# Modulation rows of a two-layer recurrent backbone: spaced differently under the mixers, a quarter under the out-projection, loaded on GpSimd's queue

## The chip, the cores and the metric

The kernel runs on one core of one Trainium2 chip. The metric is the device time of one execution in microseconds (us), the median of several runs; lower is better. The engines are TensorE (PE, with its weight loads as PEld), VectorE (DVE), ScalarE (ACT), GpSimd (POOL) and SyncE (SP). SP computes nothing here: it issues DMAs, in order, and holds at the first one whose buffer is not free yet.

## What is computed

Two layers work on 256 context tokens and 1024 latent tokens of width 1024, all in float32. Each layer is a mixing sub-layer (four groups of heads: HGRN2, mLSTM, retention, GLA, each scanned forwards and backwards, then one out-projection) and a squared-ReLU MLP. Both are modulated by vectors made from a conditioning vector, one for the latent tokens (`c`) and one for the context (`c_ctx`):

```python
def modulate(x, shift, scale):
    return rmsnorm(x) * (1.0 + scale) + shift

mod_l = (jax.nn.silu(c) @ w_ada[layer] + b_ada[layer])[:, None, :]
mod_c = (jax.nn.silu(c_ctx) @ w_ada[layer] + b_ada[layer])[None, None, :]
sh1_l, sc1_l, g1_l, sh2_l, sc2_l, g2_l = jnp.split(mod_l, 6, axis=-1)
xl = xl + g1_l * mixer_out(raw_l, pl, g_heads[layer], w_out[layer])
xl = xl + g2_l * sq_relu_mlp(modulate(xl, sh2_l, sc2_l), w_ff1[layer], w_ff2[layer])
```

## The kernel before, in words

Activations lie with the channels on the 128 partitions and the 1280 tokens along the free dimension, in three token blocks: 256 context columns, then twice 512. Every matrix product is done as three float32r products (`mm3`, lines 293 to 296), with each operand split into a high and a low part. A weight half is loaded raw by SP (line 281), its high part is copied by ACT (282), its low part is subtracted by DVE (283).

The modulation of layer 0's first sub-layer (part r = 0) is made by TensorE at the start. The other parts are made by **modulation rows** in `ada_rows`: for each token kind j, each half h of the 1024 inputs and each of 16 blocks o of 128 outputs, a DMA brings 128 rows of `w_adaR`, 512 wide (256 KB, line 413), and one DVE instruction multiplies them with the conditioning half `c` and accumulates along the free dimension (line 414). `c` is itself a DMA of `d_c`, broadcast to 128 partitions (line 410). Before the change all these DMAs stand on SP's queue, between its weight loads, stores and fetches.

Where rows are made:

- Under the mixers of layer 0 (`mixers`): parts r = 1 and 2 of layer 0, 128 rows, with two row buffers and one conditioning buffer from the heap. The mixers' own steps are generators that `Fill.along` interleaves with dense projections. Each step of a projection is a fill step, and on three of every five of them one row is emitted (`self.n % 5 in (0, 2, 4)`). The order of phases is GLA, HGRN2 (two head pairs), mLSTM, retention.
- Under the MLP of layer 0: parts r = 0, 1, 2 of layer 1, 128 rows, from the generator `ada1`, which `filler` advances three times after each of the 32 hidden tiles. It has five row buffers and one conditioning buffer, so each change of half waits until the last product with the old half is done, and then for a load.

```python
ring = Ring(ws[2 * o:2 * o + 2]) if o < fixed else rest
u = self.wtile(self.io["w_out"][l, o], ring)
```

The out-projection (`outproj`) keeps the weights of its first `fixed` output blocks in place for all three token blocks, and streams the others through a ring of three slots, again for each token block. With 13 slots `fixed` is 5.

What a line emits is only a wish: a scheduler at build time puts each engine's instructions in their final order, and may put a row's product earlier or later among DVE's instructions than its place in the program. Each engine then executes its own list strictly in that order. DVE operations of HGRN2 that matter below are the exponent differences and masked copies of `mix_vec` (lines 919 to 1038), which feed PE.

## Time and profile before

| what | value |
|---|---|
| median of 3 runs (lowest, highest) | 3276.86 us (3276.39, 3285.53) |
| the profiled execution's own time | 3277.57 us |
| its span, first to last instruction | 3275.8 us |
| mean granted TensorE clock | 0.990 |
| busy: PE, DVE, ACT, POOL | 97%, 64%, 39%, 0% |

The mixers of layer 0 take the time from about 55 to 760 us of the span, its out-projection goes on to 918 us, its MLP to about 1790 us; then layer 1 follows in the same order, without rows. PE is the engine that is nearly always busy, so what counts is where it stands idle and where its granted clock is below 1.00. The view by windows gives both for any stretch; the view of waits names what PE waited for.

### The profile page before, as it was taken

The page shows a single profiled execution, that of the slowest core. Times are in us where ns is not written, and L with a number is a line of the kernel's source. Part 1 is how long each engine was busy: PE and PEld are TensorE (multiplying, and loading weights), DVE is VectorE, ACT ScalarE, POOL GpSimd, SP SyncE. Part 2 cuts the span into 40 slices and gives each one's busy share as a digit, 9 for nine tenths or more (in the row PEclk, how much of TensorE's full clock was granted, in tenths as well). Part 3 has the DMA queues.
Part 4 walks back from the last instruction along what each step waited for, and adds up shares of the span by engine and source line. Part 5 has one row for each costly group of instructions (what it writes and reads, how often), then busy time and mean ns, then how long its engine had stood idle before and what let it go on. Part 6 is the DMA issues. An engine that isn't in the chain of part 4 may idle for free.

```text
span 3275.8 us, 52563 instructions
## 1 busy us (share of the span) xinstructions
PE 3188.0 (97%) x20681; PEld 2607.3 (80%) x20681; DVE 2098.3 (64%) x4333; ACT 1285.0 (39%) x2665; POOL 11.5 (0%) x42
## 2 busy tenths in 40 slices
PE   7999999999999999999999999999999999999998
PEld 4787788878888888888888677788778888888887
DVE  4778887776588845454545586876756555555546
ACT  4666564545332121212122575764444322222222
POOL 0000000000000000000000000000000000000000
PEclk9999899999999999999999999999999999999999
DMA  6115566345157511111111212333224111111111
GB/s 208 58 61 176 183 186 190 120 134 179 63 165 230 161 39 39 39 39 39 39 39 40 78 64 73 120 109 113 90 72 151 58 46 52 46 52 46 52 49 65
DMA packets 181953, 308.20 MB, mean 94 GB/s; under 512 B 21880, under 2 KB 51240, under 8 KB 181448
## 3 DMA queue, kind: packets, MB, share of 16 engines
q1 hardware_dynamic: 180376, 303.02, 28.8%
q8 instruction: 162, 2.65, 0.3%
q10 hardware_dynamic: 1296, 1.81, 0.2%
q14 instruction: 87, 0.71, 0.1%
q0 software_dynamic: 32, 0.01, 0.0%
HBM read 259.11 MB, written 45.65 MB: 93 GB/s over the span
## 4 chain that ended last, share of the span: by engine, by line
PE 81%; DVE 8%; DMA 6%; ACT 3%; issue 1%; SPq 0%; DVEq 0%; ACTq 0%
PE psum L294 22%; PE psum L295 21%; PE psum L296 21%; PE psum L831 2%; PE psum L601 2%; PE psum L834 1%; PE psum L818 1%; PE psum L632 1%; DMA ph<-w_adaR 1%; PE psum L634 1%; PE psum L633 1%; PE psum L1359 1%; PE psum L706 1%; PE psum L1019 1%; DMA ps<-w_ada 1%
## 5 line engine op out<-in xcount | busy, mean ns | idle before, releaser
L526 DVE SCALAR_TENSOR_TENSOR x<-psum,st,x 128x512 f32<-128x512 f32 (+1 forms) x648 | 440.7, 689 | 203.5 <-PE psum L296 202.8
L282 ACT ACTIVATE pc<-st 128x512 fp32r<-128x512 f32 x256 | 161.2, 632 | 854.4 <-PE psum L295 840.9
L295 PE MATMUL psum<-pc,pc 128*128 128x512 f32 (+1 forms) x1296 | 477.0, 368 | 6.0 <-DVE pc L506 6.0
L294 PE MATMUL psum<-pc,pc 128*128 128x512 f32 (+1 forms) x1296 | 476.1, 367 | 0.0
L296 PE MATMUL psum<-pc,pc 128*128 128x512 f32 (+1 forms) x1296 | 474.7, 366 | 0.0
L294 PE MATMUL psum<-Hhi,pc 128*128 128x512 f32 (+1 forms) x1280 | 471.1, 368 | 1.5 <-ACT pc L282 1.5
L295 PE MATMUL psum<-Hlo,pc 128*128 128x512 f32 (+1 forms) x1280 | 472.0, 369 | 0.1
L296 PE MATMUL psum<-Hhi,pc 128*128 128x512 f32 (+1 forms) x1280 | 470.5, 368 | 0.0
L294 PE MATMUL psum<-Hhi,pw 128*128 128x512 f32 (+1 forms) x1192 | 451.5, 379 | 7.6 <-ACT pw L282 3.5
L295 PE MATMUL psum<-Hlo,pw 128*128 128x512 f32 (+1 forms) x1192 | 447.5, 375 | 0.0
L296 PE MATMUL psum<-Hhi,pw 128*128 128x512 f32 (+1 forms) x1192 | 446.6, 375 | 0.6 <-DVE pw L283 0.6
L505 DVE TENSOR_TENSOR st<-st 128x256 f32<-128x256 f32 (+1 forms) x160 | 101.8, 637 | 301.5 <-ACT pc L504 300.8
L295 PEld LDWEIGHTS psum<-pc,pc 128*128 128x128 f32 x1296 | 245.0, 189 | 48.4 <-DVE pc L506 6.9
L294 PEld LDWEIGHTS psum<-pc,pc 128*128 128x128 f32 x1296 | 245.0, 189 | 44.1 <-DVE x L526 1.2
L296 PEld LDWEIGHTS psum<-pc,pc 128*128 128x128 f32 x1296 | 244.6, 189 | 42.9 <-issue 2.7
L294 PEld LDWEIGHTS psum<-Hhi,pc 128*128 128x128 f32 x1280 | 241.3, 189 | 43.3 <-ACT pc L282 2.4
L295 PEld LDWEIGHTS psum<-Hlo,pc 128*128 128x128 f32 x1280 | 241.3, 189 | 41.0 <-issue 0.5
L283 DVE TENSOR_TENSOR pc<-st,pc 128x512 fp32r<-128x512 f32 x256 | 175.6, 689 | 153.4 <-ACT pc L282 133.5
L296 PEld LDWEIGHTS psum<-Hhi,pc 128*128 128x128 f32 x1280 | 241.1, 188 | 41.0 <-DVE pc L283 0.6
L294 PEld LDWEIGHTS psum<-Hhi,pw 128*128 128x128 f32 x1192 | 227.3, 191 | 53.7 <-issue 9.2
L296 PEld LDWEIGHTS psum<-Hhi,pw 128*128 128x128 f32 x1192 | 227.1, 191 | 39.3 <-issue 2.4
L295 PEld LDWEIGHTS psum<-Hlo,pw 128*128 128x128 f32 x1192 | 227.6, 191 | 37.7 <-issue 2.9
(401 smaller groups left out, 4859.4 us busy)
## 6 DMA issues: line engine op xcount, KB each, us to landing
st<-w_ff SPq DMA_DIRECT2D x256, 256.0 KB
ph<-w_adaR SPq DMA_DIRECT2D x128, 256.0 KB
st<-w_inT SPq DMA_DIRECT2D x96, 256.0 KB
st<-w_adaR SPq DMA_DIRECT2D x74, 256.0 KB
pc<-w_adaR SPq DMA_DIRECT2D x54, 256.0 KB
st<-w_out SPq DMA_DIRECT2D x50, 256.0 KB
d_z<-st SPq DMA_DIRECT2D x40, 256.0 KB
ps<-w_ada SPq DMA_DIRECT2D x32, 256.0 KB
```

The source lines that it names most:

```text
L282: nc.scalar.activation(hi, raw, AF.Copy)
L283: (eng or nc.vector).tensor_tensor(lo, raw, F(hi), op=ALU.subtract)
L294: t.matmul(out, lhsT=w[0], rhs=m[0], start=first, stop=False)
L295: t.matmul(out, lhsT=w[0], rhs=m[1], start=False, stop=False)
L296: t.matmul(out, lhsT=w[1], rhs=m[0], start=False, stop=last)
L505: nc.vector.tensor_tensor(r, r, r, op=ALU.mult)
L526: nc.vector.scalar_tensor_tensor(x, ps, self.mod[:, l, 40 + o, j:j + 1], x, op0=ALU.mult, op1=ALU.add)
L601: t.matmul(ps[:, 0:304], lhsT=h[a], rhs=u[b], start=(k + i == 0), stop=(k == NK - 1 and i == 2))
L632: t.matmul(ps[:, e, :], lhsT=h[0], rhs=u[0], start=(k == 0), stop=False)
L633: t.matmul(ps[:, e, :], lhsT=h[0], rhs=u[1], start=False, stop=False)
L634: t.matmul(ps[:, e, :], lhsT=h[1], rhs=u[0], start=False, stop=(k == NK - 1))
L831: nc.tensor.matmul(o, lhsT=ST[r0:r0 + kd, c, d, :], rhs=qd[d](c)[r0:r0 + kd, :], start=(j == 0), stop=False, tile_position=(r0, 0))
```

## The change

Five things are altered.

1. Under the mixers a row is emitted on 5 of every 20 fill steps in HGRN2, and on 11 of 20 from mLSTM on.
2. Half of part r = 2 (output blocks 8 to 15, 32 rows for both token kinds) is left out there and made in the out-projection: none or one row after each context output, two after each 512-column output. Two slots of the out-projection are cut into two row buffers and two conditioning buffers, so that 11 slots are left and `fixed` is 4.
3. In the out-projection and in the MLP both conditioning halves are kept for as long as the token kind stays the same, and the rows alternate between the halves.
4. In the MLP the six buffers are four for rows and two for conditioning, in place of five and one.
5. All row and conditioning DMAs are issued from GpSimd's queue.

```diff
-                self.n += 1
-                if self.also and self.n % 5 in (0, 2, 4):
-                    next(self.also, None)
+                if self.also:
+                    self.due += self.part
+                    if self.due >= 20:
+                        self.due -= 20
+                        next(self.also, None)
...
-            for h in range(2):
-                c = cs.next()(512)
-                queue.dma_start(c.rearrange("p (k q) -> p k q", q=128), self.d_c[j:j + 1, 4 * h:4 * h + 4, :].to_broadcast([128, 4, 128]))
-                for o in range(16):
-                    w = wring.next()(512)
-                    queue.dma_start(w, self.io["w_adaR"][l, r, o, :, 512 * h:512 * h + 512])
-                    nc.vector.scalar_tensor_tensor(w, w, 1.0, c, op0=ALU.mult, op1=ALU.mult, accum_out=S[:, o:o + 1, h])
-                    if o % several == several - 1:
-                        yield
+            if both and self.cond_now != j:
+                self.cond_c = [cond(j, h) for h in range(2)]
+                self.cond_now = j
+            seq = [(h, o) for o in range(o0, o1) for h in range(2)] if both else [(h, o) for h in range(2) for o in range(o0, o1)]
+            for i, (h, o) in enumerate(seq):
+                if both:
+                    c = self.cond_c[h]
+                elif o == o0:
+                    c = cond(j, h)
+                w = wring.next()(512)
+                queue.dma_start(w, self.io["w_adaR"][l, r, o, :, 512 * h:512 * h + 512])
+                nc.vector.scalar_tensor_tensor(w, w, 1.0, c, op0=ALU.mult, op1=ALU.mult, accum_out=S[:, o:o + 1, h])
+                if i % several == several - 1:
+                    yield
...
-            fill.also = ada([ao.sub(512 * i, 512) for i in range(3)])
+            fill.also, fill.part = ada([ao.sub(512 * i, 512) for i in range(3)]), 5
...
+        fill.part = 11
...
-        nslot = (self.rest - NK * NT) // 1024
-        po, ws = self.pool(f"po{l}", [1024] * (nslot - 5))
+        nslot = (self.rest - NK * NT) // 1024 - (0 if l else 2)
+        po, ws = self.pool(f"po{l}", [1024] * (nslot - 5) + [512] * (0 if l else 4))
+        rows = None
+        if l == 0:
+            ab, ws = ws[-4:], ws[:-4]
+            rows = self.ada_rows(0, 2, (0, 1), Ring(ab[:2]), Ring(ab[2:]), nc.gpsimd, o0=8)
+            self.cond_now = None
...
+                if rows:
+                    for _ in range(o % 2 if a < CTX else 2):
+                        next(rows, None)
...
-            for r in (1, 2):
-                yield from b.ada_rows(0, r, (0, 1), Ring(bufs[:2]), Ring(bufs[2:]), nc.sync)
+            for r, n in ((1, 16), (2, 8)):
+                yield from b.ada_rows(0, r, (0, 1), Ring(bufs[:2]), Ring(bufs[2:]), nc.gpsimd, o1=n)
...
+            w4, c2 = Ring(bufs[:-2]), Ring(bufs[-2:])
+            b.cond_now = None
             for r in range(3) if l == 0 else ():
-                yield from b.ada_rows(1, r, (0, 1) if r == 0 else (1,), Ring(bufs[:5]), Ring(bufs[5:]), nc.sync, 2)
+                yield from b.ada_rows(1, r, (0, 1) if r == 0 else (1,), w4, c2, nc.gpsimd, 2)
```

The rest of the diff counts the rows that a part has and adds the bias for that many. Line numbers shift by two at the top (281 to 283 becomes 283 to 285) and by 13 in the middle (`mix_vec`'s line 980 becomes 993). A row's DMA is line 426 then, its product 427, a conditioning load 412.

**DVE, in the middle of HGRN2's first head pair** (the multiplications of line 991, later 1004, and the masked copies of line 1032, later 1045, belong to `mix_vec`; `ph` written together with `st` is a row's product). Before:

```order
L981 TENSOR_TENSOR px_0_693<-px_0_693 128x64x4
L414 SCALAR_TENSOR_TENSOR ph_0_256,st<-ph_0_256 128x512
L991 SCALAR_TENSOR_TENSOR px_0_693<-px_0_693,st 128x512
L414 SCALAR_TENSOR_TENSOR ph_0_256,st<-ph_0_256 128x512
L991 SCALAR_TENSOR_TENSOR px_0_693<-px_0_693,st 128x512
L742 TENSOR_TENSOR st<-st,psum 128x512
L283 TENSOR_TENSOR pw_0_252<-st,pw_0_252 128x512
L1032 COPY_PREDICATED px_0_693<-st,psum 128x256
```

With the change:

```order
L994 TENSOR_TENSOR px_0_693<-px_0_693 128x64x4
L665 TENSOR_TENSOR st<-st 128x256
L1004 SCALAR_TENSOR_TENSOR px_0_693<-px_0_693,st 128x512
L427 SCALAR_TENSOR_TENSOR ph_0_256,st<-ph_0_256 128x512
L1004 SCALAR_TENSOR_TENSOR px_0_693<-px_0_693,st 128x512
L313 SCALAR_TENSOR_TENSOR st<-psum,st 128x512
L285 TENSOR_TENSOR pw_0_252<-st,pw_0_252 128x512
L1045 COPY_PREDICATED px_0_693<-st,psum 128x256
```

Between the same neighbours one product stands where two stood.

**POOL's queue under HGRN2's second head pair** (`spill_v`'s memsets of a column of ones, line 768, later 781, are POOL's only work there before). Before, all ten stand in one row:

```order
L1210 MEMSET ph_0_256 128x16
L768 MEMSET st 128x4 x10
L1291 MEMSET px_0_693 128x65
```

With the change (around the third conditioning load):

```order
L781 MEMSET st 128x4
L426 DMA ph_0_256<-w_adaR 128x512 x3
L781 MEMSET st 128x4
L426 DMA ph_0_256<-w_adaR 128x512 x2
L412 DMA ph_0_256<-d_c 128x512
L426 DMA ph_0_256<-w_adaR 128x512 x2
L781 MEMSET st 128x4 x2
L426 DMA ph_0_256<-w_adaR 128x512 x4
```

The rows stand between memsets that wait for their own buffers.

**SP's queue at the start of the out-projection** (`x_0` to `x_7` are the residual, `w_out` the weights). Before:

```order
L281 DMA st<-w_out 128x512 x2
L1540 DMA x_6_7732<-xT 128x512
L1540 DMA x_7_7733<-xT 128x512
...
L1540 DMA x_7_7733<-xT 128x512
L281 DMA st<-w_out 128x512 x18
```

With the change:

```order
L1552 DMA st<-d_yg 128x512
L1559 DMA x_6_7670<-xT 128x512
L1559 DMA x_7_7671<-xT 128x512
...
L1559 DMA x_7_7671<-xT 128x512
L283 DMA st<-w_out 128x512 x24
```

The loads of the fifth output block's weights (two halves for each of the three token blocks, where two were enough before) now all stand behind the last residual load.

## Rows read from the trace of the kernel before

**Rows 1.** The page: span, then busy time, share and instructions of each engine.

```profile
span 3275.8 us, 52563 instructions
PE 3188.0 (97%) x20681; PEld 2607.3 (80%) x20681; DVE 2098.3 (64%) x4333; ACT 1285.0 (39%) x2665; POOL 11.5 (0%) x42
```

**Rows 2.** Windows: length, busy PE, PEld, DVE, ACT, POOL (instructions), granted clock, DMA share, GB/s.

```profile
294.00:353.00 59.00, 48.78 (x432) 36.26 (x431) 51.39 (x123) 36.04 (x77) 0.00 (x0) 0.83 0.42 135
353.00:563.00 210.00, 203.52 (x1996) 170.61 (x1997) 171.48 (x460) 118.15 (x269) 1.29 (x12) 1.00 0.61 193
563.00:641.00 78.00, 76.31 (x557) 61.38 (x555) 59.82 (x177) 38.50 (x110) 0.24 (x2) 1.00 0.47 144
641.00:691.00 50.00, 45.47 (x293) 36.36 (x291) 42.09 (x115) 25.63 (x72) 0.00 (x0) 0.90 0.44 139
...
760.00:918.00 158.00, 153.62 (x805) 128.53 (x803) 89.90 (x154) 72.26 (x135) 0.00 (x0) 0.99 0.38 125
...
1053.00:1070.00 17.00, 11.59 (x50) 9.57 (x49) 12.79 (x37) 3.61 (x6) 0.00 (x0) 0.80 0.80 243
```

**Rows 3.** PE's waits in 294:353, 641:691 and 918:1123: us in total, times, longest.

```profile
PE psum L956 <- DVE px L935: 3.9, 1, 3.9
...
PE psum L818 <- DVE ph L1135: 2.3, 1, 2.3
PE psum L294 <- DVE st L311: 1.9, 1, 1.9
...
PE psum L295 <- DVE pc L506: 5.4, 1, 5.4
```

**Rows 4.** Windows of the rows' products (line 414): length, DVE busy (instructions), clock, DMA.

```profile
294.00:353.00 59.00, 11.36 (x34) 0.83 0.42 135
353.00:563.00 210.00, 49.65 (x144) 1.00 0.61 193
```

**Rows 5.** The chain of waits in 200:760: shares by line, then pieces (start us, us).

```profile
by line: PE psum L294 12.2%; PE psum L295 11.9%; PE psum L296 11.8%; DMA ph<-w_adaR 6.9%; PE psum L831 5.2%; PE psum L834 3.6%; PE psum L818 3.1%; PE psum L1359 3.1%; DVE ph L414 2.8%; PE psum L706 2.5%; PE psum L1019 2.3%; DVE px L991 2.3%
...
411.35 3.73 DMA ph<-w_adaR
...
433.43 3.04 DMA ph<-w_adaR
```

**Rows 6.** Line 414 in 353:563: instructions, then what its engine's idle time waited for (us, times).

```profile
L414 DVE SCALAR_TENSOR_TENSOR ph<-ph x72: 680/686/695, 355.8 to 553.9; 128x512 f32<-128x512 f32 x72
...
  DMA ph<-w_adaR: 11.0, 17
  DMA ph<-d_c: 1.7, 2
```

**Rows 7.** The same of line 414 in 918:1123, the MLP.

```profile
  DMA st<-d_c: 19.0, 7
  DMA st<-w_adaR: 3.2, 8
```

**Rows 8.** Waits of SP's queue in 227:720.

```profile
SPq L413 <- DVE ph L414: 106.0, 73, 8.0
```

**Rows 9.** Timeline of POOL; landing of its one DMA (line 333); window 0:50.

```profile
24.85 0.64 POOL L333 DMA_DIRECT2D d_c<-st  x1 [24.41 <-DVE st L332]
...
420.66 0.10 POOL L768 MEMSET st<- 128x4 f32 x1 [4.92 <-DMA d_v<-st]
...
DMA to landing us min/median/max: 4.9/4.9/4.9
...
0.00:50.00 50.00, 31.63 (x133) 10.42 (x133) 16.55 (x71) 19.24 (x48) 1.20 (x7) 1.00 0.91 311
```

**Rows 10.** Waits of PE and ACT around the out-projection's first block, and SP's timeline there.

```profile
PE psum L294 <- ACT pw L282: 3.5, 2, 2.7
...
ACT pw L282 <- DMA st<-w_out: 4.5, 2, 4.0
...
809.28 5.52 SPq L1540 DMA_DIRECT2D x<-xT  x10
```

More of the change, by code (lines that the diff above doesn't have):

```diff
@@ L161, in __init__ @@
         self.slots = slots
-        self.q, self.done, self.owed, self.also, self.n = [], 0, 0, None, 0
+        self.q, self.done, self.owed, self.also, self.part, self.due = [], 0, 0, None, 0, 0
     def add(self, *work):
@@ L400, in ada_finish, with ada_rows, cond @@
             nc.vector.tensor_scalar(m, m, 1.0, None, op0=ALU.add)
-    def ada_rows(self, l, r, toks, wring, cs, queue, several=1):
+    def ada_rows(self, l, r, toks, wring, cs, queue, several=1, o0=0, o1=16):
         nc = self.nc
         S = self.mod[:, 1 - l, 0:16, :]
-        for j in toks:
-            for h in range(2):
-                c = cs.next()(512)
-                queue.dma_start(c.rearrange("p (k q) -> p k q", q=128), self.d_c[j:j + 1, 4 * h:4 * h + 4, :].to_broadcast([128, 4, 128]))
-                for o in range(16):
-                    w = wring.next()(512)
-                    queue.dma_start(w, self.io["w_adaR"][l, r, o, :, 512 * h:512 * h + 512])
-                    nc.vector.scalar_tensor_tensor(w, w, 1.0, c, op0=ALU.mult, op1=ALU.mult, accum_out=S[:, o:o + 1, h])
-                    if o % several == several - 1:
-                        yield
-            mo = self.mod[:, l, 16 * r:16 * r + 16, j]
-            nc.vector.tensor_tensor(mo, S[:, :, 0], S[:, :, 1], op=ALU.add)
-            nc.vector.tensor_tensor(mo, mo, self.bada[:, l, 16 * r:16 * r + 16], op=ALU.add)
-            if r in (0, 2):
+        def cond(j, h):
+            c = cs.next()(512)
+            queue.dma_start(c.rearrange("p (k q) -> p k q", q=128), self.d_c[j:j + 1, 4 * h:4 * h + 4, :].to_broadcast([128, 4, 128]))
+            return c
+        both = len(cs.items) > 1
+        for j in toks:
+            if both and self.cond_now != j:
[12 more added lines that the diff above has]
+                    yield
+            mo = self.mod[:, l, 16 * r + o0:16 * r + o1, j]
+            nc.vector.tensor_tensor(mo, S[:, o0:o1, 0], S[:, o0:o1, 1], op=ALU.add)
+            nc.vector.tensor_tensor(mo, mo, self.bada[:, l, 16 * r + o0:16 * r + o1], op=ALU.add)
+            if (r, o0) in ((0, 0), (2, 0)):
@@ L1566, in outproj @@
                 nc.vector.scalar_tensor_tensor(x, ps, self.mod[:, l, 16 + o, j:j + 1], x, op0=ALU.mult, op1=ALU.add)
+                if rows:
+                    for _ in range(o % 2 if a < CTX else 2):
+                        next(rows, None)
             if a != tbs[-1][0]:
                 self.norm_block(l, (a, n), 24, 32, fast=FAST[4])
+        for _ in rows or ():
+            pass
         po.release()
```

## The prediction

> **What bounds the kernel now.** I read the page first. PE is busy for 3188.0 of 3275.8 us [rows 1], so a change can only win where PE stands idle or runs at a lower clock; DVE, at 64% of the whole, seems to have room. But its share is an average, so the next view is the table of windows, cut where the clock falls [rows 2]. From 294 to 353 us, in HGRN2's first head pair, DVE is busy for 51.39 of 59 us, PE for only 48.78, and the granted clock is 0.83. From 641 to 691, in mLSTM's end and retention's start, PE is busy for 45.47 of 50 at 0.90. From 1053 to 1070, in the MLP, PE is busy for 11.59 of 17 at 0.80. These three short stretches are what the rows of modulation can be charged with; the view of PE's waits says why: in all three PE waits for DVE, 3.9 us at once in the first and 5.4 in the third [rows 3]. A clock below 1.00 is time at the lower level, 1.2 GHz in place of 2.4; in each stretch it follows such a wait.
>
> The reader should see next that the rows are in DVE's way twice. Their products take 11.36 us of DVE in the first stretch and 49.65 in the following 210 us [rows 4], and they make DVE wait for their DMAs: 11.0 us in 17 waits there [rows 6]. The chain of waits from 200 to 760 us runs through row DMAs for 6.9% and through products for 2.8% [rows 5]. In the MLP most of the waiting, 19.0 us, is for the conditioning load `d_c` [rows 7].
>
> The sums are made against the profiled execution's own 3277.57 us; the median of the three runs is 0.7 lower. What a measurement of this kernel can tell from no change is about 0.3%, 9.8 us.
>
> **Where the rows go.** Counting products between the same neighbours in the two orders on DVE, I find 10 before 294 us (11 with the change), 16 against 5 in 294 to 353, 73 against 78 in 353 to 563, 7 against 2 in 563 to 641, 13 against none in 641 to 691, and 9 against none after that; 96 remain. So the emission at 5 of 20 steps does not thin out all of HGRN2: the scheduler pulls the later rows forward, into its second half, and clears mLSTM and retention.
>
> **294 to 353 us.** PE's idle time is 59 - 48.78 = 10.2 us, and the clock's shortfall 0.17 x 59 = 10.0, of which 3.9 / 2 = 1.9 falls on the long wait itself and is not lost twice: 8.1. A product costs 49.65 / 72 = 0.69 us. Eleven fewer free 7.6 us of DVE. I take it that PE's idle time shrinks by those 7.6, three quarters of it, and the clock's loss by the same share, 6.0: gain **13.6**, bounds 0 (the wait has another cause) and 18.3.
>
> **563 to 691 us.** The second stretch loses 4.5 us idle and 0.10 x 50 = 5.0 by the clock. All 13 products leave it, so I take 9 of the 9.5. From 563 to 641 PE idles 1.7 us, and five of seven products go: 1. Gain **10**, bounds 0 and 11.2.
>
> **MLP.** Eight conditioning loads through one buffer become four through two. The third stretch loses 5.4 us idle and 0.20 x 17 = 3.4 by the clock. I take **6** of these 8.8, because one change of token kind keeps its load; bounds 0 and 8.8. The row ring falls from five buffers to four. Four buffers give a row every (4.0 + 0.69) / 4 = 1.2 us with the trip assumed below, and 128 rows in the 205 us from 918 to 1123 need one every 1.6, so I cost that at nothing; at the 4.9 us below it still fits (1.4).
>
> **The other queue.** Taking rows off SP frees it of 106.0 us in which it held for a row's buffer [rows 8]. I give that no gain of its own: no wait of PE in these rows ends on a load. On POOL's queue a row is issued behind memsets, and one of these waited 4.92 us for a store [rows 9]; a product then holds DVE, and with it the operations that feed PE. The price that the trace does not show is a row's round trip from POOL. On SP's queue it is 3.04 to 3.73 us where nothing else held it [rows 5]; POOL's only DMA took 0.64 us to issue and 4.9 to land, though to device memory and with the DMA engines 0.91 busy [rows 9]. I take 4.0, nearer to SP's rows because the transfer is the same, and keep 3.04 and 4.9 as bounds.
>
> With two buffers the 78 rows of 353 to 563 come in 39 pairs, and each waits some 0.6 us longer: 23 us. Six conditioning loads there have only two to eight DVE operations between the last product with the old half and the first with the new, where four to thirteen stood before; at 2 us each that is 12. So 35 us of DVE waits replace 12.7 [rows 6]. DVE's work is 171.48 + 5 x 0.69 = 175 of the 210 us, so 35 just fit, but not without harm, as DVE works in order. PE idles 6.5 us there now beside 12.7 of waits, half a microsecond for each; 22 more cost **-11**. Bounds: 0 (trip 3.4 or less) and -41 (trip 4.9: 39 x 1.5 + 6 x 3 = 76.5 of waits, 41.5 more than DVE has free).
>
> The Trainium skill, page “DMA: Bandwidth & Descriptors”, section “Latency and other measured facts”, puts the first byte at about 1 us where GpSimd's software makes the descriptors and 0.6 where hardware does. By its 0.4 us the pairs would wait 16 us, the loads still 12, and the sum would be 3256; no run here shows it yet.
>
> **Out-projection.** Four more weight halves cost DVE 4 x 0.69 us and 32 products 22, all beside 68 us in which DVE idles [rows 2]; without that cover they would cost up to 25. Streamed weights are late in the first block: PE waits 2.7 us once for a copy that waits 4.0 for `w_out`, behind ten residual loads that SP issues over 5.52 us [rows 10]. With the change four context outputs and one of 512 columns stand ahead of that wait, where there were five and two thirds of one, about 1 us less of cover; the load comes some 0.7 earlier, as one pair fewer is ahead. I take **-1**, bounds +2 and -6 (the wait doubles, and so does the clock's loss, 0.01 x 158).
>
> **Sum:** 13.6 + 10 + 6 - 11 - 1 = 17.6 us gained: 3260.0 for the profiled execution, **3259** for the median.
>
> **Rivals.**
>
> *The load only moves.* DVE in 353 to 563 goes from 82% to 83% by work alone and to the brim with waits; the stall of 294 to 353, which came at 87%, then returns a hundred microseconds later. For it: the 78 products there. Against it: 73 stand there already and PE lost 6.5 us. It takes back the 13.6: **3273**, no change.
>
> *All gain, no price.* If POOL's trip is as SP's and the loads are covered, the gains at their upper bounds are 18.3 + 11.2 + 8.8 = 38.3: **3239**. For it: rows no longer hold behind stores on SP. Against it: closer conditioning loads.
>
> *Slower: the trip from POOL.* Of one pair's 210 / 39 = 5.4 us the trip may take 4.7 before two buffers starve DVE. With a trip of 4.9 the 41 us above are lost, and the time is 3277.6 - 29.6 + 1 + 41 = **3290**. It decides at 4.8: there the waits are 39 x 1.4 + 18 = 73 us, 38 over DVE's 35 free, which is the gain of 28.6 and the 9.8 that count. For it: the 4.9 us of the one row there is. Against it: its destination and its crowded engines. The Trainium skill's page “SBUF — State Buffer”, section “SBUF: two separate sides”, has a mechanism that would lengthen the trip: while DVE runs an operation that takes both shared ports, GpSimd cannot write descriptors. No row here shows it.
>
> **How the numbers follow.** Forecast 0.44 (3249 to 3267), the load moves 0.24 (3268 to 3286), all gain 0.17, slower 0.15. Faster by over 0.3% is the first and third, less a hundredth for the forecast's edge: 0.60; the same 0.25; slower 0.15. The range runs from the full gain, 3238, to the upper end of no change, 3287, and leaves out the slow case alone.
>
> **What would show it.** Right: in the new profile the clock stays at 1.00 around 294 to 353 and 641 to 691, PE's waits for lines 935 and 1135 (by their new numbers) are gone or under 1 us, the MLP's waits for `d_c` fall under 6 us, and DVE's waits for row DMAs before 563 are near 35 us. Wrong: a new stretch below 0.9 of the clock between 353 and 563, or in the out-projection; a landing time of POOL's row DMAs above 4.8 us; or a wait on `d_c` that has grown in HGRN2.

## The result, and the profile after the change

The change is slower: 3304.24 us, the median of four runs (3299.94 to 3306.91), against 3276.62 for the kernel before in the same comparison. The ratio is 1.0081, its 95% interval 1.0066 to 1.0097; that is 26.5 us, and lies outside the range of the forecast. The profiled execution took 3303.77 us.

The page of the change, the rows that answer to [rows 1]:

```profile
span 3302.0 us, 52653 instructions
...
PE 3197.7 (97%) x20681; PEld 2617.5 (79%) x20681; DVE 2104.3 (64%) x4341; ACT 1287.3 (39%) x2669; POOL 157.3 (5%) x314
```

PE's idle time has grown from 87.8 us to 3302.0 - 3197.7 = 104.3, by 16.5 of the 26.2 us of span. The mean granted clock fell from 0.990 to 0.988; its shortfall is 39.6 us in place of 32.8. The two together make 23 of the 26 (time in which PE idles at the lower clock is in both). DVE's share hasn't moved: where the time went does not show in shares.

To see where, I lined the traces up by PE's work. Both hold the same 20681 matmuls; each is counted with its form's median duration in the trace before, and at a given amount of work done the two times are compared. The table says how many us later than the kernel before a kernel reaches that point (negative: earlier), with the points named by the time before. The lines below that of the change belong to the experiments. Each line is one execution, so small differences say little: f3_gpsimd and f3_mix, the same program up to the MLP, differ by 2.7 us at 775 (-8.5 and -11.2), and between 1227 us and the end, where no edit reaches, a line still moves by up to 4.5 us (f3_gpsimd).

| kernel | 304 | 357 | 493 | 570 | 672 | 775 | 890 | 1227 |
|---|---|---|---|---|---|---|---|---|
| the change | +5.9 | -8.9 | -1.2 | +11.4 | +17.5 | +9.0 | +21.2 | +25.8 |
| u_queue | +0.8 | -8.6 | -9.1 | -3.7 | -2.9 | -11.6 | -3.8 | -7.0 |
| f_gpsimd | +1.1 | -7.2 | -2.4 | +8.6 | +9.4 | +0.8 | +15.8 | +22.0 |
| o_space | -1.1 | -10.5 | -10.7 | -4.8 | -4.5 | -11.0 | -5.7 | -6.1 |
| s_noout | -1.8 | -10.7 | -12.5 | -6.6 | -6.5 | -12.8 | -7.2 | -10.5 |
| s3_noout | 0.0 | -10.3 | -16.7 | -17.6 | -17.8 | -25.1 | -26.9 | -29.4 |

Up to 775 us the mixers run, up to 890 most of the out-projection, up to 1227 the part of the MLP that has rows. In the change the gain of HGRN2's first pair is there: from 304 to 357 us it wins 14.8. It is lost again, and more, between 357 and 672 us (26.4), partly won back (8.5), and then 12.2 go in the out-projection and 4.6 in the MLP.

Windows of the change, cut where its clock falls (columns as in [rows 2]):

```profile
264.00:294.00 30.00, 27.57 (x227) 20.19 (x225) 21.79 (x72) 18.01 (x49) 3.22 (x6) 1.00 0.65 211
294.00:353.00 59.00, 57.39 (x521) 46.18 (x521) 53.54 (x121) 45.64 (x103) 3.75 (x7) 1.00 0.39 128
...
495.00:528.00 33.00, 22.69 (x299) 19.35 (x297) 26.43 (x67) 13.10 (x24) 8.03 (x15) 0.83 0.52 162
528.00:563.00 35.00, 32.79 (x290) 28.53 (x291) 22.93 (x75) 13.80 (x35) 8.49 (x16) 0.87 0.48 147
563.00:641.00 78.00, 75.25 (x534) 60.69 (x532) 57.19 (x166) 39.58 (x110) 2.46 (x7) 0.96 0.48 154
641.00:691.00 50.00, 49.57 (x305) 39.73 (x304) 38.65 (x101) 23.55 (x68) 0.00 (x0) 1.00 0.31 90
781.00:939.00 158.00, 144.32 (x717) 121.53 (x715) 106.22 (x216) 68.14 (x126) 19.80 (x37) 0.97 0.57 185
1074.00:1093.00 19.00, 12.60 (x57) 10.25 (x56) 15.53 (x43) 3.61 (x6) 8.05 (x15) 0.92 0.79 246
```

The two stretches that the forecast wanted to clear are clear: 57.39 of 59 us and 49.57 of 50, both at 1.00. A new one stands at 495 to 528: PE is busy for 22.69 of 33 us at 0.83, and the clock is still at 0.87 behind it. The out-projection, as long a window as in [rows 2], has PE idle for 13.7 us where it was 4.4.

PE's waits in 495:528, 781:939 and 1020:1095 of the change (us in total, times, longest):

```profile
PE psum L1032 <- DVE px L1004: 8.4, 4, 4.8
...
PE psum L451 <- DVE st L449: 4.6, 2, 2.9
PE psum L296 <- DVE st L664: 3.6, 1, 3.6
...
PE psum L297 <- DVE pc L519: 8.9, 2, 6.4
```

The waits shown name DVE operations that aren't rows: line 1004 is the one that stands between products in the order quoted above. Two more waits in 781:939, 5.4 us, end on ACT. In DVE's timeline, products that hold for their DMA, or several products in a row, stand ahead of most of them: of the two waits for line 449, one is behind a product that held for 2.02 us, the other has no product near it. The wait of 6.4 us in the MLP shows it best; these are the last products ahead of it (four of the six that stand in a row from 1083.7 us on; start us, us, engine, instruction, in brackets the wait), and PE's instruction that waits:

```profile
1085.39 0.69 DVE L427 SCALAR_TENSOR_TENSOR pc<-pc,st 128x512 f32<-128x512 f32 x1 [0.24 <-DMA pc<-w_adaR]
...
1086.74 0.69 DVE L427 SCALAR_TENSOR_TENSOR st<-st 128x512 f32<-128x512 f32 x1 [0.66 <-DMA st<-w_adaR]
...
1088.46 0.69 DVE L427 SCALAR_TENSOR_TENSOR st<-st 128x512 f32<-128x512 f32 x1 [1.02 <-DMA st<-w_adaR]
...
1089.12 0.69 DVE L427 SCALAR_TENSOR_TENSOR pc<-pc,st 128x512 f32<-128x512 f32 x1
...
1090.95 0.69 DVE L519 TENSOR_TENSOR pc<-st,pc 128x512 fp32r<-128x512 f32 x1
...
1091.69 0.79 PE L297 MATMUL psum<-pc,pc 128*128 128x512 f32 x1 [6.40 <-DVE pc L519]
```

The view of line 427, the product, says how long DVE held, for the mixers, the out-projection and the MLP in turn:

```profile
  DMA ph<-w_adaR: 27.2, 32
  DMA ph<-d_c: 7.7, 5
...
  DMA po<-w_adaR: 22.2, 20
...
  DMA pc<-w_adaR: 10.6, 14
  DMA st<-w_adaR: 8.2, 12
  DMA st<-d_c: 3.7, 1
```

In the mixers DVE waits 34.9 us. The forecast's 35 were for 353 to 563 us alone; there it is 24.7 (before: 12.7):

```profile
  DMA ph<-w_adaR: 18.7, 25
  DMA ph<-d_c: 6.0, 4
```

And there are 22.2 more in the out-projection, where the forecast had none, and in the MLP row waits have grown from 5.4 to 18.8 while `d_c` fell from 19.0 to 3.7.

### The profile page after: what moved, and what is told of

The parts are those of the page before. It is cut to its first block, busy times and chain, and to the rows that moved or that the text cites. A ratio compares the mean times of both kernels' runs of the same rounds, so it can differ in the third digit from the quotient of the medians.

```text
span 3302.0 us, 52653 instructions
## 1 busy us (share of the span) xinstructions
PE 3197.7 (97%) x20681; PEld 2617.5 (79%) x20681; DVE 2104.3 (64%) x4341; ACT 1287.3 (39%) x2669; POOL 157.3 (5%) x314
## 4 chain that ended last, share of the span: by engine, by line
PE 62%; DVE 4%; issue 3%; ACT 1%; POOL 1%; DMA 1%; SPq 0%; POOLq 0%; DVEq 0%; ACTq 0%
PE psum L296 18%; PE psum L297 18%; PE psum L298 18%; PE psum L844 1%; PE psum L645 1%; PE psum L647 1%; PE psum L614 1%; PE psum L646 1%; POOL st L426 1%; PE psum L831 1%; POOL pc L426 1%; PE psum L847 1%; PE psum L1032 0%; PE psum L1372 0%; DVE st L490 0%
## 5 line engine op out<-in xcount | busy, mean ns | idle before, releaser
L296 PE MATMUL psum<-Hhi,pw 128*128 128x512 f32 (+1 forms) x1216 | 459.6, 378 | 2.5 <-ACT pw L284 2.5
L298 PE MATMUL psum<-Hhi,pw 128*128 128x512 f32 (+1 forms) x1216 | 455.8, 375 | 0.0
L297 PE MATMUL psum<-Hlo,pw 128*128 128x512 f32 (+1 forms) x1216 | 454.8, 374 | 0.0
L296 PEld LDWEIGHTS psum<-Hhi,pw 128*128 128x128 f32 x1216 | 231.4, 190 | 49.0 <-issue 9.7
L298 PEld LDWEIGHTS psum<-Hhi,pw 128*128 128x128 f32 x1216 | 231.1, 190 | 40.0 <-issue 2.5
```

Of the source, the lines that this page charges most:

```text
L296: t.matmul(out, lhsT=w[0], rhs=m[0], start=first, stop=False)
L297: t.matmul(out, lhsT=w[0], rhs=m[1], start=False, stop=False)
L298: t.matmul(out, lhsT=w[1], rhs=m[0], start=False, stop=last)
```

## The experiments

Four theories stood at the start: the queue (a row takes longer from GpSimd), the rows in the out-projection, the MLP's smaller ring, and the spacing itself. Ratios below are to the kernel before on the same chip; a thousandth is 3.3 us.

| run | what it is | us | ratio (95%) |
|---|---|---|---|
| the change | | 3304.2 | 1.0081 (1.0066 to 1.0097) |
| u_queue | rows on SyncE | 3267.8 | 0.9974 (0.9963 to 0.9986) |
| u_out | out-projection as before | 3295.8 | 1.0059 (1.0040 to 1.0077) |
| u_mlp | MLP buffers as before | 3305.4 | 1.0090 (1.0074 to 1.0107) |
| u_space | 12 of 20 throughout | 3297.9 | 1.0069 (1.0054 to 1.0084) |
| o_queue | before, queue alone | 3295.2 | 1.0057 (1.0042 to 1.0072) |
| o_space | before, spacing alone | 3271.6 | 0.9979 (0.9965 to 0.9994) |
| s_noout | SyncE, spacing and MLP | 3270.0 | 0.9984 (0.9975 to 0.9993) |
| s_slots | s_noout, 11 weight slots | 3270.0 | 0.9978 (0.9969 to 0.9988) |
| f_gpsimd | GpSimd, order of u_queue | 3292.6 | 1.0049 (1.0034 to 1.0063) |
| f_sync | SyncE, order of the change | 3313.9 | 1.0116 (1.0089 to 1.0143) |
| q3 | the change, 3 row buffers | 3293.3 | 1.0057 (1.0041 to 1.0072) |
| s3_noout | s_noout, 3 row buffers | 3251.5 | 0.9924 (0.9899 to 0.9950) |
| o_s3 | before, 3 row buffers | 3276.6 | 1.0001 (0.9987 to 1.0016) |
| s3_thin | s3_noout, thinner MLP rows | 3255.6 | 0.9933 (0.9917 to 0.9950) |
| f3_gpsimd | GpSimd, order of s3_thin | 3273.7 | 0.9978 (0.9964 to 0.9992) |
| f3_mix | the same, mixers' rows only | 3261.4 | 0.9958 (0.9942 to 0.9975) |
| f3_mlp | the same, MLP's rows only | 3256.9 | 0.9947 (0.9930 to 0.9963) |

### Undoing one part

**u_queue** (the same edit at the three places where a queue is given):

```diff
-                yield from b.ada_rows(0, r, (0, 1), Ring(bufs[:2]), Ring(bufs[2:]), nc.gpsimd, o1=n)
+                yield from b.ada_rows(0, r, (0, 1), Ring(bufs[:2]), Ring(bufs[2:]), nc.sync, o1=n)
```

> The change with all its row and conditioning DMAs back on SyncE's queue; spacing, out-projection rows and MLP buffers as in the change. Theory A (the queue itself costs little: a row lands 3.4 us after its issue from GpSimd, as from SyncE): within 5 us of the change's 3304, that is 3299 to 3309, and DVE's waits for rows under the mixers stay near 35 us. Theory B (the trip from GpSimd is what costs, as the prediction's term of 11 us has it): 3304 - 11 to - 25, that is 3279 to 3293, with DVE's waits for rows under the mixers down to some 15 us. Theory C (SyncE holds for row buffers and is late with weights and stores): above 3309.

It came below all three, at 3267.8: with the rows back on SyncE the whole loss is gone, 0.0107 or 35 us. (The build also orders the program otherwise then; that is parted below.) What is left of the change is faster than the kernel before by a quarter of a per cent. Waits for rows under the mixers fell to 10.4 us in 13 waits, so theory B has the direction, not the size.

**u_out** (the rows' generator in the out-projection is taken out with it):

```diff
-        nslot = (self.rest - NK * NT) // 1024 - (0 if l else 2)
+        nslot = (self.rest - NK * NT) // 1024
...
-            for r, n in ((1, 16), (2, 8)):
+            for r, n in ((1, 16), (2, 16)):
```

> The change with its out-projection as before: all 128 rows under the mixers again, 13 weight slots, fixed 5. Theory A (the 12 us that are lost between 775 and 890 us come from the 32 rows and four more weight halves there, and the 32 rows cost less under the mixers): 3288 to 3296, with PE's idle time in the out-projection under 5 us. Theory B (the rows take as much where they are put back): 3298 to 3310.

3295.8, at the upper edge of A; its interval overlaps that of the change. PE idles 5.2 us in 781:939, where A wanted under 5 and the change has 13.7. In the line-up the out-projection costs 0.2 us then in place of 12.2, but the mixers stand at +14.9 at 775 us in place of +9.0: half of it is paid where the rows are put back.

**u_mlp**:

```diff
-                yield from b.ada_rows(1, r, (0, 1) if r == 0 else (1,), w4, c2, nc.gpsimd, 2)
+                yield from b.ada_rows(1, r, (0, 1) if r == 0 else (1,), Ring(bufs[:5]), Ring(bufs[5:]), nc.gpsimd, 2)
```

> The change with five row buffers and one conditioning buffer in the MLP, halves one after the other, still on GpSimd's queue. Theory A (the fourfold ring costs: row waits went from 5.4 to 18.8 us when the fifth buffer went): 3296 to 3301, the wait of 6.4 us near 1085 us gone. Theory B (the fifth buffer is worth nothing and the loads of d_c cost as before): 3302 to 3312, with 15 to 20 us of DVE waits for d_c in the MLP.

Theory B: 3305.4, with 19.1 us of waits for `d_c`. In the line-up the MLP loses 9.3 us in place of 4.6. The fifth buffer is not what is missing; two conditioning buffers are worth it on this queue too.

**u_space**:

```diff
-            fill.also, fill.part = ada([ao.sub(512 * i, 512) for i in range(3)]), 5
+            fill.also, fill.part = ada([ao.sub(512 * i, 512) for i in range(3)]), 12
...
-        fill.part = 11
+        fill.part = 12
```

> The change with a row on 12 of every 20 fill steps throughout the mixers, as before; the 96 rows there, the rest as in the change. Theory A (the sparser rows give back between 493 and 672 us what they gain before and after): 3297 to 3309. Theory B (the prediction's: the spacing is worth 13.6 + 10 us): 3320 to 3330, with PE's clock below 0.9 around 300 us again. Theory C (the spacing is itself what loses): 3285 to 3296.

Theory A: 3297.9. On GpSimd's queue the sparser rows are worth nothing; the gain that they bring from 304 to 357 us (14.8 in the change, 3.1 here) is given back behind it.

### One part alone

**o_queue** is the kernel before with `nc.gpsimd` at its two calls of `ada_rows`, and nothing else.

> The kernel before with nothing altered but the queue: all row and conditioning DMAs on GpSimd's. Theory A (the longer way from a product's end to the next row, some 0.5 us more from GpSimd, is paid wherever two buffers must turn fast, so the queue alone loses): 3276 + 20 to + 36, that is 3296 to 3312. Theory B (the queue only hurts together with the rows in the out-projection and the sparser emission): 3270 to 3285.

3295.2, a microsecond under A's interval and far from B. The queue costs 19 us by itself and 35 in the change.

**o_space** is the kernel before with the new counting of the emission and its values 5 and 11 alone, rows on SyncE.

> The kernel before with the spacing alone (5 and 11 of 20), on SyncE's queue, MLP and out-projection as before. By the line-up of s_noout against before the MLP part is worth 3.3 us (889 to 1227 us), so s_noout + 3: 3271 to 3276, and about 10 us are gained before 775 us against the kernel before; by the prediction's 6 for the MLP part, 3275 to 3279.

3271.6, in the first interval. The spacing is worth 7 us by the ratio. By the line-up it gains 9.4 from 304 to 357 and 6.5 from 672 to 775 us, and gives back 5.9 from 493 to 570 and 5.3 from 775 to 890, with the out-projection as before.

**s_noout** joins the edits of u_queue and u_out.

> Spacing and MLP part of the change, rows on SyncE's queue, out-projection as before with all 128 rows under the mixers. Theory A (in u_queue the stretch from 775 to 890 us is 7.8 us longer than before, and that goes): 3254 to 3265. Theory B (the 32 rows cost as much under the mixers): 3266 to 3276.

Theory B: 3270.0, the same as u_queue. On SyncE's queue, then, it makes no difference that can be measured where the 32 rows are. It isn't a kernel without rows in the out-projection, though: with the sparser emission the last 14 of its 128 products run from 759.9 to 790.5 us, at the out-projection's start, where they hold DVE for 7.8 us, and PE waits there for the copy of a weight:

```profile
PE psum L296 <- ACT po L284: 5.2, 1, 5.2
```

The clock falls there for 6.8 us. o_space has the same 14 products and a wait of 4.8 us. How much of that the rows make no run shows.

**s_slots** leaves the slots cut and the rows under the mixers:

```diff
         if l == 0:
-            ab, ws = ws[-4:], ws[:-4]
-            rows = self.ada_rows(0, 2, (0, 1), Ring(ab[:2]), Ring(ab[2:]), nc.sync, o0=8)
-            self.cond_now = None
+            ws = ws[:-4]
```

> As s_noout, but the out-projection keeps the change's 11 weight slots and fixed 4, and leaves the four buffers unused; no rows there. Theory A (the rows and the waits that they bring hold VectorE there, the slots cost nothing): within 2 us of s_noout. Theory B (four more weight halves that are streamed are what costs): s_noout + 4 to + 8 us.

Theory A: 3270.0 both. Four more weight halves cost nothing.

### Trip or order

Moving the DMAs to another queue also changes what the build makes of the program: of the 4085 places in DVE's list (the readings of sums left out), 951 hold another operation in the change than in u_queue. To part the two, the next kernels carry a table of another kernel's order, and tie each instruction of DVE, PE and ACT to the one ahead of it. Everything that these three engines execute then stands in the same order as there; the traces show it so. SyncE's list isn't tied: of its 1021 other DMAs 4 stand elsewhere in f_gpsimd than in u_queue, 42 in f_sync than in the change.

```diff
+            if last is not None:
+                tc.add_manual_dep(i, last.name, mybir.DependencyInfo(mybir.DependencyClass.NoSync, mybir.DependencyReason.DATA), reason="order")
+            last = i
...
         build(ctx, tc, io)
+        same_order(nc, tc)
```

**f_gpsimd**:

> Rows on GpSimd's queue as in the change, but VectorE, TensorE and ScalarE execute their instructions in exactly the order that the build gave to u_queue (a table of that order is added as ordering edges without waits). Theory A (the trip of a row from GpSimd is what costs the 36 us between u_queue and the change): 3295 to 3310. Theory B (the build answers to the other queue with a worse order, and that is what costs): 3266 to 3276. Something between says how much of each.

**f_sync**:

> The reverse: rows on SyncE's queue, but VectorE, TensorE and ScalarE in exactly the order of the change. Theory A (the trip): 3266 to 3276. Theory B (the order): 3296 to 3308.

| ratio | rows on SyncE | rows on GpSimd |
|---|---|---|
| order of u_queue | 0.9974 | 1.0049 |
| order of the change | 1.0116 | 1.0081 |

f_gpsimd came between the two theories: in one order the queue costs 0.0075, 24.6 us, and the change's own order 0.0032, 10.5 us, more. With intervals of some 0.0015 on each ratio, both are good to about 7 us. f_sync is slower than both: each order fits the queue that it was made for. So the 24.6 us are the queue's price in u_queue's order and not in every order: in that of the change GpSimd is the faster queue, by 0.0035, just beyond the noise. In f_sync's trace rows on SyncE take 14.0, 15.5 and 16.2 us from the last product of their buffer to the next, and PE waits 11.3 us at once. SyncE holds them behind other DMAs: in the second case the buffer is free at 570.6 us and the row is issued at 579.4, after seven other DMAs, at one of which (line 1490) SyncE held for 4.7 us until PE was done with its buffer.

With the order fixed the same 96 products of the mixers can be compared one by one. Here is one of them, first in u_queue (start us, us, engine, instruction, and in brackets its wait; the first two rows are the last product in the same buffer and the reading of its sum, the third is SyncE's row DMAs, three together, the last the product that waits):

```profile
509.72 0.68 DVE L427 SCALAR_TENSOR_TENSOR ph<-ph 128x512 f32<-128x512 f32 x1
510.33 0.08 DVE L427 DVE_READ_ACCUMULATOR ph<-ph 128x1 f32 x1
...
510.44 3.65 SPq L426 DMA_DIRECT2D ph<-w_adaR  x3
...
513.04 0.69 DVE L427 SCALAR_TENSOR_TENSOR ph<-ph 128x512 f32<-128x512 f32 x1 [0.69 <-DMA ph<-w_adaR]
```

and in f_gpsimd, with POOL's DMA:

```profile
519.83 0.68 DVE L427 SCALAR_TENSOR_TENSOR ph<-ph 128x512 f32<-128x512 f32 x1
520.43 0.08 DVE L427 DVE_READ_ACCUMULATOR ph<-ph 128x1 f32 x1
...
520.81 0.54 POOL L426 DMA_DIRECT2D ph<-w_adaR  x1 [1.75 <-DVE ph L427]
...
523.80 0.69 DVE L427 SCALAR_TENSOR_TENSOR ph<-ph 128x512 f32<-128x512 f32 x1 [0.88 <-DMA ph<-w_adaR]
```

From the end of the reading to the next product in that buffer: 513.04 - 510.41 = 2.63 us on SyncE, 523.80 - 520.51 = 3.29 on GpSimd. Of it, SyncE begins to issue 0.03 us after the buffer is free and POOL 0.30 after; SyncE's issues take 0.33 us at the median, POOL's 0.54. In the ten products before 720 us that wait for their row in both kernels after a turn under 6 us, GpSimd's turn is longer by 0.45 us at the median (from 0.5 shorter to 0.7 longer), which is about what the two parts make, 0.27 and 0.21. What it does to DVE, line 427 of u_queue:

```profile
  DMA po<-w_adaR: 18.2, 15
  DMA ph<-w_adaR: 10.4, 13
  DMA pc<-w_adaR: 8.2, 12
  DMA ph<-d_c: 4.9, 3
  DMA st<-d_c: 3.5, 1
  DMA st<-w_adaR: 2.9, 7
```

and of f_gpsimd:

```profile
  DMA po<-w_adaR: 24.5, 18
  DMA ph<-w_adaR: 22.9, 26
  DMA pc<-w_adaR: 13.1, 16
  DMA ph<-d_c: 8.1, 5
  DMA st<-w_adaR: 7.9, 13
  DMA st<-d_c: 3.9, 1
```

80.4 us in place of 48.1, in the mixers (`ph`), the out-projection (`po`) and the MLP (`pc`, `st`) alike. 32.3 us more of DVE's waits cost 24.6 us of time, three quarters of a microsecond each.

### A third row buffer

If two buffers expose the trip, a third should hide it. There is room for it:

```diff
-        ao = hp.alloc(1536, True) if l == 0 else None
+        ao = hp.alloc(2048, True) if l == 0 else None
...
-            fill.also, fill.part = ada([ao.sub(512 * i, 512) for i in range(3)]), 5
+            fill.also, fill.part = ada([ao.sub(512 * i, 512) for i in range(4)]), 5
...
-                yield from b.ada_rows(0, r, (0, 1), Ring(bufs[:2]), Ring(bufs[2:]), nc.gpsimd, o1=n)
+                yield from b.ada_rows(0, r, (0, 1), Ring(bufs[:3]), Ring(bufs[3:]), nc.gpsimd, o1=n)
```

**q3** has this edit on the change, **s3_noout** on s_noout, **o_s3** on the kernel before.

> The change with a third row buffer under the mixers (512 more columns of the heap), all else as in the change, rows on GpSimd's queue. Theory A (the trip from GpSimd is exposed by two buffers): the waits for rows under the mixers fall from 27 to under 12 us, and most of the 20 us that the mixers lose against u_queue come back: 3280 to 3292. Theory B (the loss has another cause, the build-time order or something in GpSimd's transfers): 3297 to 3308.

> As s_noout (spacing and MLP part, SyncE's queue, out-projection as before), with a third row buffer under the mixers. If rows still hold VectorE there, the 23 us of waits fall under 10 and the time to 3258 to 3266, below both kernels; if those waits have cover, 3267 to 3273.

> The kernel before with nothing but a third row buffer under the mixers. If two buffers are what makes rows hold VectorE, most of s3_noout's 18 us over s_noout comes here too: 3256 to 3266. If the third buffer only helps where the rows are sparser: 3268 to 3277.

In all three the build makes its own order, and no run holds the order between two buffers and three; what is the buffer's and what the order's stays open. q3 came between its theories at 3293.3. Its mixers stand at -0.3 us at 775 where the change has +9.0 and u_queue -11.6, so 9.3 of the 20.6 us are back; row waits there fell from 27.2 to 16.5 us, above the 12 that were expected, and those for `d_c` grew to 14.1. Its loss from 493 to 570 is not gone (15.2 us, with a fall of the clock for 17 us at 553.6). s3_noout did better than expected: 3251.5 us, the fastest kernel of the study, 0.0060 below s_noout. Its row waits under the mixers are 5.9 us in 9, and the windows are clean but for the first:

```profile
294.00:353.00 59.00, 55.50 (x482) 43.23 (x481) 53.94 (x128) 43.94 (x93) 0.00 (x0) 0.94 0.43 139
353.00:495.00 142.00, 139.92 (x1431) 116.19 (x1430) 124.00 (x325) 84.74 (x189) 1.06 (x10) 1.00 0.63 199
495.00:563.00 68.00, 67.15 (x639) 57.80 (x638) 50.19 (x154) 32.20 (x90) 0.31 (x2) 1.00 0.51 160
```

The stretch behind 495 us, where every sparser kernel with two buffers loses (5.9 us in o_space, 12.6 in the change), is gone. That is 6.8 of the 18.9 us by which the line-up parts s3_noout from s_noout at 1227. Another 7.4 lie between 775 and 890: in s3_noout the last product under the mixers starts at 750.7 us, and no row is left for the out-projection. o_s3, the third buffer without the spacing, is worth nothing (1.0001), though its row waits fell to 4.7 us: from 294 to 353 us PE is busy for 48.86 of 59 us at a clock of 0.86, as before. That the products themselves crowd that stretch is likely and not shown. On SyncE the two gain together what neither gains alone.

**s3_thin** spreads the MLP's rows:

```diff
-            for _ in range(3):
+            for _ in range(3 if next(tiles) % 4 == 0 else 2):
```

> s3_noout (spacing, MLP conditioning per token, third row buffer under the mixers, SyncE's queue, out-projection as before) with the MLP's rows thinner: 2 or 3 steps of the row generator after a hidden tile (3 on every fourth) in place of 3. If the rows' bunching fills VectorE in the MLP, the wait of 3.3 us near 1034 us and its half clock go: 3244 to 3250. If not, 3250 to 3254.

3255.6, a little above the second interval, and no gain (0.9933 and 0.9924, intervals overlap): the wait is still there, at 1041 us, 3.9 long. Thinner emission did not thin out what DVE executes at that place.

### What the queue costs when there is slack

These take s3_thin's order as a table, and put all rows (**f3_gpsimd**), those of the mixers (**f3_mix**) or those of the MLP (**f3_mlp**) on GpSimd's queue.

> Rows on GpSimd's queue, with VectorE, TensorE and ScalarE in exactly the order of s3_thin. Theory A (the half microsecond more per row is all there is, and a third buffer and thinner rows cover it): s3_thin + 2 to + 9 us, with under 4 us lost in the mixers where f_gpsimd lost 12.4, and DVE's waits for rows some 10 to 15 us up, not 32. Theory B (GpSimd's transfers cost in another way): s3_thin + 18 to + 30 us.

> The order of s3_thin frozen, the mixers' rows on GpSimd's queue, the MLP's on SyncE's. If the stages add up as the line-up of f3_gpsimd has it: s3_thin + 12 us, 3265 to 3270. If the third buffer covers the trip in the mixers and the rest was chance of the clock: s3_thin + 0 to + 5. In the new trace a fall of the clock near 496 and 551 us, as in f3_gpsimd, says that it is the queue's doing.

> The order of s3_thin frozen, the MLP's rows on GpSimd's queue, the mixers' on SyncE's. By the line-up of f3_gpsimd the MLP takes 7.6 us of the loss: s3_thin + 5 to + 10 us, with waits for rows in the MLP near 21 us where s3_thin has 14, and a wait of PE near 1050 us of 6 to 7 us where s3_thin has 3.9.

By the ratios f3_gpsimd is 14.7 us slower than s3_thin, f3_mix 8.2 and f3_mlp 4.6. The last two are hardly or not clear of noise (their intervals overlap that of s3_thin); they add up, 12.8 against 14.7, within it. f3_mix came between its two cases, f3_mlp just under its 5. DVE's waits grew by 12.6 us (from 28.9 to 41.5), as theory A had it, but its price is missed: about one microsecond for each, and 14.7 lies between the theories. In f3_mlp row waits in the MLP are 20.4 us (s3_thin 14.0), and PE's longest wait there is 5.2 us (3.9). Theory A's under 4 us lost in the mixers is missed too: the line-up at 775 us has 11.7 between f3_gpsimd and s3_thin, 9.0 for f3_mix, where two buffers lost 12.4. The trip brings 5.6 us of waits there in f3_gpsimd and 9.6 in f3_mix with three buffers, where it brought 15.7 with two (f_gpsimd against u_queue): a part is covered, and what is left is dearer apiece. The ties themselves cost nothing that shows: f3_mlp, which is s3_thin with ties up to 890 us, stands at -22.7 at 775, s3_thin at -20.2.

The falls of the clock at 496 and 551 us, of 6.8 us each in f3_gpsimd, were asked for in f3_mix. PE waits near 496 us as before; the wait and the window of 490:510, f3_gpsimd first, then f3_mix:

```profile
PE psum L969 <- DVE px L1045: 2.1, 1, 2.1
...
490.00:510.00 20.00, 17.93 (x167) 14.31 (x166) 13.48 (x34) 5.07 (x9) 3.23 (x6) 0.83 0.51 161
```

```profile
PE psum L969 <- DVE px L1045: 2.1, 1, 2.1
...
490.00:510.00 20.00, 17.08 (x177) 13.73 (x176) 16.61 (x44) 6.80 (x13) 4.94 (x10) 1.00 0.64 196
```

The same wait of 2.1 us, of the same instruction in the same order and on the same queue; once the clock falls to its lower level and once not. With the mixers' rows on SyncE it is the same: in f3_mlp the clock falls for 3.4 us at 491.1, after a wait of 1.2 us of that instruction,

```profile
PE psum L969 <- DVE px L1045: 1.2, 1, 1.2
...
485.00:500.00 15.00, 13.81 (x123) 10.92 (x122) 10.87 (x29) 4.58 (x9) 0.00 (x0) 0.89 0.54 172
```

and in s3_thin, in the same order, it stays at 1.00 after one of 1.7. So the fall near 496 is not the queue's doing alone; it followed some of these waits and not others, on either queue. A part of the differences between single executions is of this kind.

## Why the prediction was wrong

Two steps failed, and neither alone would have led out of the range: what is not the queue gained 8.5 us where 28.6 were counted, and the queue with its order took 35.1 where 11 were.

**The other queue, -11: the first step that failed.** Its mechanism was right: the trip is half a microsecond longer (0.6 was taken), and in one order the queue costs the mixers 0.8 + 11.6 = 12.4 us at 775 (11). That these two numbers are near is in part luck. The forecast had 22 us more of waits at half a microsecond each; f_gpsimd has 15.7 more than u_queue (31.0 against 15.3), and they cost 0.8 each. In the change's own 353 to 563 us the waits are 24.7 us and not 35, but PE idles for 20.0 us there where it was 6.5, and its clock falls to 0.83. The price of a wait was mis-sized.

It was also charged to one stage. In the MLP the prediction said "I cost that at nothing", since four buffers give a row every 1.2 us and one is needed every 1.6; in the out-projection the products lay "beside 68 us in which DVE idles". The line-up of f_gpsimd against u_queue has 7.2 us there, and 9.4 in the MLP. Both covers were averages. DVE's list has products in bunches, six in a row from 1083.7 to 1089.8 us in the change, where PE waits 6.4 us, and an operation that PE needs stands behind the bunch: idle time elsewhere in the stage does not help it. In one order the queue makes PE's waits for that operation (line 519) 7.5 us in the MLP in place of 3.1 (f_gpsimd, u_queue).

**The spacing, 13.6 + 10: the second step that failed.** Alone, on SyncE, it is worth 6.9 us (o_space). The gains were counted where they arise, as if the time stayed won. They arise, 9.4 from 304 to 357 us and 6.5 from 672 to 775, but 5.9 are lost again from 493 to 570, where the products now stand, and 5.3 from 775 to 890, where the last 14 rows of o_space run.

**A term was missing: the order.** The change's own order costs 10.5 us more on GpSimd's queue than u_queue's. I read its orders and counted products, but priced only the counts.

**294 to 353, 13.6.** Place and size are right: from 304 to 357 us the change gains 14.8 us. But 4.3 of them had been lost just ahead, between 264 and 304, and on SyncE (u_queue, o_space) it is 9.4.

**563 to 691, 10.** The second half came (8.5 us from 672 to 775 in the change, 6.5 in o_space), the first turned over: 6.1 us lost from 570 to 672 in the change, none in o_space.

**The rival "the load only moves"** was right in part: every sparser kernel with two buffers stalls anew between 505 and 527 us. With rows on SyncE it costs 5.4 to 5.9 us, and s3_noout's third buffer removes it; on GpSimd it costs 12.6, and q3 with its third buffer still loses 15.2. Its price of all 13.6 was too much on SyncE and about right on GpSimd.

**MLP, +6.** On SyncE it is 3.3 us in the line-up (s_noout, 890 to 1227) against 0.4 for o_space, and no difference by the ratios; on GpSimd 4.7 (u_mlp against the change). About half of the six by the line-up, near what one execution can tell, and smaller than what the queue takes there.

**Out-projection, -1.** The slots cost nothing (s_slots). The term as a whole was too small even on SyncE: from 775 to 890 us u_queue loses 7.8 us in the line-up, beyond the bound of 6, while s3_noout, with no row there, gains 1.8. That u_queue and s_noout are equal in time does not speak for it, as s_noout has rows left over there and loses 5.6. On GpSimd it is 12.2 us in place, of which u_out gives back 7 in all.

The sum by these measured terms: what is not the queue gains 8.5 us (u_queue; the forecast had 13.6 + 10 + 6 - 1 = 28.6), the queue in one order takes 24.6 (forecast 11), its own order 10.5 (no term): 26.6 lost, and 26.5 were measured. The three are steps between the same ratios, so that they meet the total is no proof of them.

**The rival "slower"** named the right part by the wrong point. It wanted a trip of 4.8 us, as only then two buffers starve DVE; the median landing is 3.4, and one turn of the buffer is 3.3 in the rows above. Its point counted DVE's free time over 210 us. Half a microsecond was enough, because PE pays for a wait when it happens, at three quarters to one microsecond each, and not the half that I took from the trace before.

**What the prediction asked for** was seen, on both sides: clock 1.00 in both old stretches, waits of PE for lines 935 and 1135 (948 and 1148 now) under 1 us, waits for `d_c` in the MLP at 3.7 us. DVE's waits for row DMAs before 563 are 24.2 us, with `d_c` 31.9, where about 35 were named. As signs of being wrong there are a new stretch below 0.9 between 353 and 563, and waits for `d_c` grown there from 1.7 to 6.0. The landing time, 3.4 us at the median, and the out-projection's clock, 0.97, gave no sign.

One reading was loose: the clock does not fall behind the long waits in the kernel before but within them. Its falls at 335.4, 680.2 and 1062.5 us lie inside the waits of PE that end at 339.0, 680.3 and 1065.9.

On the Trainium skill's page “DMA: Bandwidth & Descriptors”, section “Latency and other measured facts”: its 0.4 us between the two kinds of descriptors is near the 0.45 measured. The prediction's sum by it, 3256, shows that the trip's length was not the error. Of the Trainium skill's page “SBUF — State Buffer”, section “SBUF: two separate sides”, where a VectorE operation that takes both shared ports locks GpSimd out of writing descriptors: the issues of all 256 rows took 0.54 us, none over 0.57, so no such lock is seen in the issues of this kernel. Why some landings took up to 6.9 us was not traced.

## What to carry to other kernels

When a transfer's trip grows, price it at every place where its ring turns, and ask at each what stands behind the waiting instruction in its engine's list; an idle share of the stage is no cover. Moving work to another queue also makes another program order: hold the order fixed in one experiment before the queue is blamed or praised. And try the smallest slack first: here one more row buffer of 256 KB beside the sparser rows and the MLP's two conditioning buffers, with the DMAs left on SyncE, gained 0.76% (3251.5 us), more than any part of the change. And look where the last piece of spread work ends: 14 of 128 rows ran into the next stage.

## What was not expected of the hardware

GpSimd's queue moves a 256 KB row about as well as SyncE's once it is under way: the turns differ by 0.45 us at the median, and the difference at the start makes as much, 0.30 against 0.03 us from the release of a buffer to the issue, and 0.54 against 0.33 for the issue itself. And TensorE's clock did not answer to the same wait in the same way: after 2.1 us of idling at one and the same instruction it fell in one execution and stayed at its upper level in the other (rows on GpSimd), and on SyncE it fell after 1.2 us and stayed up after 1.7.
